# Another order of the experts in a mixture-of-experts layer, and the bias products one place later

## The chip, the cores and the metric

The kernel runs on one core of a Trainium2 chip. The metric is the device time of one execution in microseconds (us). Before the change the median of three runs is 1303.01 us (1302.18 to 1307.84).

## The reference, cut to what matters

One decoder layer on 512 tokens of 1024 channels, all in float32. A mixer (a causal convolution group beside a group of attention heads) is followed by a layer norm, and then by a mixture of experts:

```
logits = x1 @ router_w + router_b            # 32 experts
top4, gates = softmax over the 4 largest logits of each token
for each expert e, on the tokens that chose it:
    g = x1 @ w_gate[e] + b_gate[e];  u = x1 @ w_up[e] + b_up[e]
    h = (clip(u) + 1) * min(g, 7) * sigmoid(1.702 * min(g, 7))
    y = h @ w_down[e] + b_down[e]
out = layer_norm(2**0.25 * x1 + sum over the 4 experts of gate * y)
```

Each expert has three 1024 x 1024 float32 matrices, 12.58 MB. All 32 are read, 403 MB of the 442 MB that the kernel moves.

## The kernel before, in words

The first 271 us compute the mixer, the first layer norm and the router; the change does not touch them. Then comes a loop over 32 places (line 1490 on, `for i, (p, rows) in enumerate(order)`). The experts are sorted by their number of tokens on the chip, and rank p of that order gets a fixed number of rows, `NBLK[p]`. A row is a block of 32 token slots: rank 0 has three, then five ranks have four, seven have three, fifteen two, four one, 78 rows in all. A place is a position in time; `TURNS` says, digit by digit, how many rows the expert at each place has, and `plan()` takes the next free rank with that number. Rows fill groups of four in the order of the places (21 groups); a group can so begin in one place and end in the next.

`expert()` works on a place in six steps. In steps c = 0 to 3 a piece of the gate and up matrices (256 input channels of both, 2.1 MB) is multiplied with the transposed tokens of every row (line 1084); ahead of it stand the bias products of the row (line 1081). After step 3 VectorE and ScalarE compute the activation (`swiglu`, lines 1065 to 1070) and write `hT`. Steps 4 and 5 take a piece of the down matrix each (line 1110 for two rows of one group side by side, line 1113 for a row alone), and the results are copied out as a high and a low part, `yh` and `yl`.

The weights come through SP's queue alone, in the order of the places, six pieces for each place (`expert_loads`, lines 303 and 312). They go to a ring of seven buffers; a piece is issued when the piece seven before it has been used (`advance`). `last_load` (line 1181) takes one of the buffers for good, for the down biases and the rows of the last layer norm: it stands in the stream ahead of the pieces of place `LASTC`, and the ring has six buffers from there.

After each step `tick(c)` lets other work in. At steps 0 and 1 the slots of later groups are worked out (`middle`, `finish`, with the gathers on GpSimd's queue). `fill()` runs one step of the sums: `combine` first makes the selections `cg` on VectorE and then, in eight steps, multiplies them with `yh` and `yl` of two groups, four matmuls of 512 columns a step (line 1154, two matmuls for a single group), and adds the result to `acc`. A combine is put on the list `combs` when the groups are complete. How many steps run is set by `FILLS`: three after step 3 for places of one or two rows, two after steps 0 and 1 for larger ones; in the last places before the end, three after every step. A forced rule clears a combine early when its buffers are wanted again. If the list is empty, nothing runs there. `add_bias` is put on the same list at the end of place `LASTC`: seven steps with the products of the gates with the down biases (line 1339) and the broadcast of the last layer norm's rows (line 1346), 24 matmuls in all. The last place, 31, has one row; the rest of the sums is done in its step 0, and the last layer norm (`outputs`) in steps 1 to 3.

Of the kernel before, what the change touches and what calls it, by code (L numbers as in the profile page):

```python
# [18 lines left out]
T, D, H, E, NE, TOPK = 512, 1024, 8, 64, 32, 4  # L19
# [12 lines left out]

TURNS = "32222422422242223331324231433211"


def plan():

    by = {n: [p for p in range(1, NE) if NBLK[p] == n] for n in (4, 3, 2, 1)}  # L40
    seq = [0] + [by[int(n)].pop(0) for n in TURNS[1:]]
    rows, n = [], 0
# [38 lines left out]
CTAIL, JORD = 4, (4, 5, 6, 7, 0, 1, 2, 3)  # L81
BANKS = (2, 2, 2, 1, 1)
RANK0 = 3.0
LASTC = NE - 4
WARM0, WARM1 = 4, (2, 2, 7)
WARM2 = (0, 0, 0, 14, 0, 0)
XBANKS = ("pu", "pu", "ps", "ps", "pt", "pt", "pu", "pu")
# [2 lines left out]
FILLS = {False: (0, 0, 0, 3, 0, 0), True: (2, 2, 0, 0, 0, 0)}  # L90
# [175 lines left out]
def tile_layer(ctx: ExitStack, tc: tile.TileContext, x, positions, w_in, conv_w, conv_b, conv_ln_g,  # L266
# [792 lines left out]
    def swiglu(st, r, ps):  # L1059
# [10 lines left out]
        V.transpose(st["hT"][:, r].rearrange("p b t -> p (b t)"), um)  # L1070

    def expert(tag, rows, sel, tick, pool=(gd, "gd"), small=lambda: None, keep=False):

        ps = [pool[0].tile([128, 2, 256], F32, name=pool[1]) for _ in rows]
        bv = bT.rearrange("p g (h q j) -> p g h q j", h=2, q=4)
        for c in range(4):
            w = got[tag, "gu", c].rearrange("p g k (h q j) -> p k g h q j", h=2, q=4)
            for i, (st, r) in enumerate(rows):
                if c == 0:
                    for q in range(4):  # L1080
                        P.matmul(ps[i][q * 32:(q + 1) * 32], sel[0:96], bv[:, :, :, q], start=True, stop=False)  # L1081
                for k in range(2):
                    for q in range(4):
                        P.matmul(ps[i][q * 32:(q + 1) * 32], st["xT"][:, r, c * 2 + k], w[:, k, :, :, q], start=False,  # L1084
                                 stop=(c == 3 and k == 1))
                if c:
                    small()
                if c == 3:
                    swiglu(st, r, ps[i])
            advance()  # L1090
            tick(c)
# [10 lines left out]
        for c in range(2):  # L1102
            w = got[tag, "dn", c].rearrange("p k (b q c) -> p k q b c", b=4, q=4)
            for u_, (st, r, n) in enumerate(units):
                d = ds_[u_]
                for k in range(4):
                    kw = dict(start=(c == 0 and k == 0), stop=(c == 1 and k == 3))
                    for j in range(4):
                        if n == 2:
                            P.matmul(d[j * 32:(j + 1) * 32], st["hT"][:, r + j % 2, c * 4 + k],  # L1110
                                     w[:, k, 2 * (j // 2):2 * (j // 2) + 2], **kw)
                        else:
                            P.matmul(d[j * 32:(j + 1) * 32, 0:256], st["hT"][:, r, c * 4 + k], w[:, k, j], **kw)  # L1113
            advance()
            tick(4 + c)
# [25 lines left out]
    def combine(sts):  # L1141

        parts = []
        for st in sts:
            cg = mw.tile([128, T], F32R, name="cg")
            V.tensor_scalar(cg, iota1, st["tk"][:, 0:1], None, op0=OP.is_equal)  # L1146
            parts += [(cg, st[y], st["used"] * 32) for y in ("yh", "yl")]
        yield
        for tt in range(TT):
            for hf in range(2):  # L1150
                c = slice(hf * 512, (hf + 1) * 512)
                ps = cb.tile([128, 512], F32, name="cb")
                for j, (cg, y, n) in enumerate(parts):
                    P.matmul(ps, cg[0:n, tt * 128:(tt + 1) * 128], y[0:n, c], start=(j == 0), stop=(j == len(parts) - 1))  # L1154
                V.tensor_tensor(acc[:, tt, c], acc[:, tt, c], ps, OP.add)  # L1155
                yield
# [31 lines left out]

    stream.insert(len(stream) - 6 * (NE - 1 - LASTC) - 6, last_load)
    GS, combs = {}, []  # L1190

    def begin(i):

        return [(g, s_) for g in range(len(GS), last_group(i) + 1)
                for s_ in [slots(members[g], lambda p, tt: rk1[:, tt, p:p + 1], lambda p, tt: aux[:, tt, p])]
                if next(s_, 0) is None]

    def middle(new):
        for g, s_ in new:
            next(s_)  # L1200

    def finish(new):
        for g, s_ in new:
            GS[g] = dict(next(s_), g=g)

    def ready_x(n):
        for g in range(n + 1):
            if "xT" not in GS[g]:
                xpose(GS[g])

    def fill():
        while combs:
            combs[0][2] -= 1
            if next(combs[0][0], 0) is None:
                return
            combs.pop(0)

    def last_group(i):
        return order[min(i, NE - 1)][1][-1][0]
# [106 lines left out]
    def add_bias():  # L1326

        t = got["last"]
        GT = mw.tile([128, T], F32, name="cg")
        ps = cb.tile([128, 512], F32, name="cb")  # L1330
        for tt in range(TT):
            P.transpose(ps[0:NE, tt * 128:(tt + 1) * 128], Gf[:, tt], ident)
        V.tensor_copy(GT[0:NE], ps[0:NE])
        bdp = t[0:NE, 0].rearrange("p (b q c) -> p q b c", b=4, q=4)
        yield
        for tt in range(TT):
            for hf in range(2):
                ps = cb.tile([128, 512], F32, name="cb")
                P.matmul(ps, GT[0:NE, tt * 128:(tt + 1) * 128], bdp[:, 2 * hf:2 * hf + 2], start=True, stop=True)
                c = slice(hf * 512, (hf + 1) * 512)  # L1340
                V.tensor_tensor(acc[:, tt, c], acc[:, tt, c], ps, OP.add)
            yield
        for i in range(4):
            c = slice(i % 2 * 512, (i % 2 + 1) * 512)
            ps = cb.tile([128, 512], F32, name="cb")
            P.matmul(ps, one1, t[0:1, 2 + i // 2, c], start=True, stop=True)
            S.activation(t[:, i // 2, c], ps, AF.Copy)
            if i % 2:
                yield
# [9 lines left out]
    def overflow():  # L1359

        pcs = cb.tile([128, 512], F32, name="cb")
        for tt in range(TT):
            P.matmul(pcs[:, 0:NE], onesb, mp[:, tt], start=(tt == 0), stop=(tt == TT - 1))
        V.tensor_tensor(ov[:, 0], pcs[:, 0:NE], cap, OP.subtract)
        V.tensor_scalar(ov[:, 1], ov[:, 0], 0.0, None, op0=OP.is_gt)
        for r in range(1, 4):
            V.scalar_tensor_tensor(ov[:, 1], ov[:, 0], 128.0 * r, ov[:, 1], op0=OP.is_gt, op1=OP.add)

        V.tensor_copy(ov[:, 2], ov[:, 1])
        for sft in (1, 2, 4, 8, 16):  # L1370
            V.tensor_copy(ov[:, 3], ov[:, 2])
            V.tensor_tensor(ov[:, 2, sft:NE], ov[:, 3, sft:NE], ov[:, 3, 0:NE - sft], OP.add)
        V.tensor_tensor(ov[:, 1], ov[:, 2], ov[:, 1], OP.subtract)
        V.tensor_copy(nit, ov[0:1, 2, NE - 1:NE])
        yield
# [114 lines left out]
    for i, (p, rows) in enumerate(order):  # L1490
        def tick(c):

            if c == 0:
                middle(new)
            if c == 0 and i == 1:
                combs.append([overflow(), (), 9])
            if c == 1:
                finish(new)
                new.clear()
            if c == 4:  # L1500
                ready_x(last_group(i + 1))
            if c == 5:
                new.extend(begin(i + 1 + LOOK))
            fills = FILLS[len(rows) > 2] if i < NE - 3 else (3, 3, 3, 3, 3, 3)
            if c == 0 and combs and combs[0][1] and combs[0][2] == 9:

                fill()
            if c < 2 and any(g - 3 in k[1] for k in combs for g, r in rows if "yh" not in GS[g]):

                for _ in range(min(3, combs[0][2] - sum(fills[c:]))):  # L1510
                    fill()
            for _ in range(fills[c]):
                fill()

        if i + 1 < NE:
            expert(p, [(GS[g], r) for g, r in rows], selr[:, p] if p else sel0, tick, small=lambda: next(first, 0))
        else:
            break
        if i == LASTC:
            combs.append([add_bias(), (), 9])  # L1520

        ready = order[i + 1][1][0][0] if i + 1 < NE - 1 else ngrp - 1
        while done < ready:
            n = 2 if done < ngrp - 3 else 1
            if done + n > ready:
                break
            combs.append([combine([GS[g] for g in range(done, done + n)]), range(done, done + n), 9])
            done += n
# [64 lines left out]
```

## Time and profile before

| | |
|---|---|
| median of three runs | 1303.01 us |
| profiled execution | 1306.11 us, its span 1304.4 us |
| TensorE (PE) busy | 1227.5 us, 94% of the span |
| VectorE (DVE), ScalarE (ACT), GpSimd (POOL) busy | 46%, 21%, 14% |
| weights queue | 429.98 MB, 81.6% of the 16 DMA engines' span |
| mean granted clock of TensorE | 0.97 of 2.4 GHz |

Start of some places, in us from the start of the span, as the first bias product of the place begins: 2 at 339.2, 3 at 363.3, 6 at 460.3, 8 at 512.0, 12 at 633.0, 16 at 755.1, 17 at 794.3, 19 at 865.4, 21 at 919.1, 22 at 945.4, 26 at 1065.8, 27 at 1117.8, 28 at 1150.9, 29 at 1188.2, 30 at 1228.8, 31 at 1252.0. The rows that each place has are the digits of the old `TURNS`, counted from 0: place 26 has four.

How to read it: busy time counts an instruction from its start to its end, and matmuls overlap, so a busy TensorE can still be slowed by its clock. PEclk is the granted clock, 1.00 for 2.4 GHz and 0.50 for 1.2 GHz. A wait is shown in brackets with what ended it. In a window the columns after the length are the busy us of TensorE's matmuls, TensorE's weight loads, VectorE, ScalarE and GpSimd, with instruction counts, then PEclk, the busy share of the DMA engines and the rate in GB/s.

### The profile page before, as it was taken

Reading aid. Unit: us, or ns where it says so; the run is one execution under the profiler, and the core shown is the slowest. Engines: PE = TensorE matmul, PEld = TensorE weight load, DVE = VectorE, ACT = ScalarE, POOL = GpSimd, SP = SyncE. Lnnn points to the kernel's source line nnn. Section 1 sums busy time; section 2 is a strip of 40 time slices with the busy share of each in tenths; the row PEclk is TensorE's granted clock in tenths of the full one; section 3 lists DMA queues with packets and bytes.
Section 4 is the critical chain, followed back from the end, with each engine's and each line's share of the span. In section 5 each row is a group of like instructions: output and inputs, shape, how many; then the busy total and the mean of one; then the engine's idle time right before and its main releaser. Section 6 shows DMA issues by size and latency. Waiting matters only on the chain. (4 is left out here: it accounts for less than half of the span.)

```text
span 1304.4 us, 25419 instructions
## 1 busy us (share of the span) xinstructions
PE 1227.5 (94%) x10578; PEld 581.5 (45%) x10578; DVE 606.1 (46%) x1444; ACT 280.4 (21%) x551; POOL 185.3 (14%) x158
## 2 busy tenths in 40 slices
PE   8989999889899999999999899999999999999984
PEld 7767767623233343343344334343435334533332
DVE  6999855743433333342333423344234444324464
ACT  5677782311000010010010001110101110101122
POOL 2854101312011011011001110001101101000002
PEclk9999999879899999999999999999999999999877
DMA  9400324679999999999999999999999999899781
GB/s 293 160 1 1 129 82 173 242 279 377 420 420 419 422 419 421 423 415 419 422 419 420 417 419 422 414 405 419 419 421 410 419 422 419 320 351 368 304 362 68
DMA packets 68658, 441.94 MB, mean 339 GB/s; under 512 B 8279, under 2 KB 16615, under 8 KB 27580
## 3 DMA queue, kind: packets, MB, share of 16 engines
q1 hardware_dynamic: 64748, 429.98, 81.6%
q0 software_dynamic: 3792, 10.29, 2.3%
q8 instruction: 85, 1.39, 0.4%
q14 instruction: 33, 0.27, 0.1%
HBM read 435.99 MB, written 4.33 MB: 338 GB/s over the span
## 5 line engine op out<-in xcount | busy, mean ns | idle before, releaser
L1084 PE MATMUL gd<-wt,xTg 128*32 128x512 f32 x4304 | 505.9, 599 | 7.4 <-DMA wt<-in_exp_w_up_dram 5.1
L1084 PEld LDWEIGHTS gd<-wt,xTg 128*32 128x32 f32 x4304 | 158.2, 111 | 288.2 <-issue 268.4
L1110 PE MATMUL gd<-wt,hT 128*32 128x512 f32 x1472 | 192.4, 602 | 15.3 <-DVE hT L1070 12.6
L1020 POOL DMA_INDIRECT xg<-x1d,idx x78 | 74.4, 954 | 864.7 <-DVE tk L1049 820.8
L1066 ACT ACTIVATE sg<-gm 128x256 f32<-128x256 f32 x78 | 32.5, 417 | 618.1 <-DVE gm L1065 616.0
L1065 DVE TENSOR_SCALAR gm<-gd 128x256 f32<-128x256 f32 x77 | 30.9, 402 | 217.1 <-PE gd L1084 211.0
L1128 DVE TENSOR_TENSOR yl<-gd,wh 32x256 fp32r<-32x256 f32 (+1 forms) x104 | 53.4, 513 | 143.3 <-ACT wh L1126 142.3
L1110 PEld LDWEIGHTS gd<-wt,hT 128*32 128x32 f32 x1472 | 58.6, 111 | 130.3 <-issue 95.7
L1126 ACT ACTIVATE wh<-gd 32x256 fp32r<-32x256 f32 (+1 forms) x104 | 46.8, 450 | 195.0 <-PE gd L1110 135.2
L548 PE MATMUL bk<-wt,wh 128*128 128x512 f32 (+1 forms) x352 | 81.2, 378 | 1.4 <-ACT sg L592 0.7
L1155 DVE TENSOR_TENSOR acc<-acc,cb 128x512 f32<-128x512 f32 x88 | 57.6, 678 | 49.9 <-PE cb L1154 49.7
L1113 PE MATMUL gd<-wt,hT 128*32 128x256 f32 x1056 | 73.0, 392 | 4.6 <-issue 2.5
L1084 PE MATMUL gd<-wb,xTg 128*32 128x512 f32 x624 | 76.7, 593 | 0.0
L548 PEld LDWEIGHTS bk<-wt,wh 128*128 128x128 f32 x352 | 61.1, 188 | 14.7 <-ACT sg L592 1.4
L586 DVE SCALAR_TENSOR_TENSOR bk<-u,cT,bk 128x512 f32<-128x512 f32 x88 | 66.2, 753 | 1.8
L1154 PE MATMUL cb<-yl,cg 128*128 128x512 f32 (+2 forms) x160 | 64.7, 404 | 0.0
L1113 PEld LDWEIGHTS gd<-wt,hT 128*32 128x32 f32 x1056 | 42.4, 113 | 32.6 <-issue 15.5
L1154 PE MATMUL cb<-wh,cg 128*128 128x512 f32 (+2 forms) x112 | 48.2, 431 | 5.9 <-DVE cg L1146 5.9
L1081 PE MATMUL gd<-wl,selr 96*32 96x512 bf16 x296 | 49.1, 385 | 0.0
L548 PE MATMUL bk<-wt,wl 128*128 128x512 f32 (+1 forms) x176 | 41.7, 379 | 2.5 <-DVE wl L539 2.1
L1069 DVE SCALAR_TENSOR_TENSOR um<-um,tk,sg 128x256 f32<-128x256 f32 x78 | 39.7, 509 | 8.9
L1128 DVE TENSOR_TENSOR yl<-gd,wl 64x512 fp32r<-64x512 f32 (+1 forms) x36 | 20.5, 570 | 48.8 <-ACT wl L1126 48.5
(340 smaller groups left out, 1292.6 us busy)
## 6 DMA issues: line engine op xcount, KB each, us to landing
wt<-in_exp_w_gate_dram SPq DMA_DIRECT2D x112, 1024.0 KB
wt<-in_exp_w_up_dram SPq DMA_DIRECT2D x112, 1024.0 KB
wt<-in_exp_w_down_dram SPq DMA_DIRECT2D x52, 2048.0 KB
wb<-in_exp_w_down_dram SPq DMA_DIRECT2D x12, 2048.0 KB
wb<-in_exp_w_gate_dram SPq DMA_DIRECT2D x16, 1024.0 KB
wb<-in_exp_w_up_dram SPq DMA_DIRECT2D x16, 1024.0 KB
wt<-in_w_in_dram SPq DMA_DIRECT2D x3, 2048.0 KB
acc<-in_x_dram SPq DMA_DIRECT2D x8, 512.0 KB
```

What stands on the lines that cost most here:

```text
L548: P.matmul(b.t[:, ts], w.t[:, k], xx[:, k, ts], start=(pas == 0 and k == 0), stop=(pas == 2 and k == KT - 1))
L586: op("V", 0.663, (lambda j: lambda e: V.scalar_tensor_tensor(b.t, u[:, c, j:j + T], cT[:, c, j:j + 1], b.t, op0=OP.mult, op1=OP.add))(j), ...
L1020: G.indirect_dma_start(out=xg[:, r], out_offset=None, in_=x1d[:, :], in_offset=bass.IndirectOffsetOnAxis(ap=idx[:, r:r + 1], axis=0))
L1069: V.scalar_tensor_tensor(um, um, st["tk"][:, 8 + r:9 + r], sg, op0=OP.mult, op1=OP.mult)
L1081: P.matmul(ps[i][q * 32:(q + 1) * 32], sel[0:96], bv[:, :, :, q], start=True, stop=False)
L1084: P.matmul(ps[i][q * 32:(q + 1) * 32], st["xT"][:, r, c * 2 + k], w[:, k, :, :, q], start=False, stop=(c == 3 and k == 1))
L1110: P.matmul(d[j * 32:(j + 1) * 32], st["hT"][:, r + j % 2, c * 4 + k], w[:, k, 2 * (j // 2):2 * (j // 2) + 2], **kw)
L1113: P.matmul(d[j * 32:(j + 1) * 32, 0:256], st["hT"][:, r, c * 4 + k], w[:, k, j], **kw)
L1126: S.activation(st["yh"][o], a, AF.Copy)
L1128: V.tensor_tensor(st["yl"][o], a, st["yh"][o].bitcast(F32), OP.subtract)
L1154: P.matmul(ps, cg[0:n, tt * 128:(tt + 1) * 128], y[0:n, c], start=(j == 0), stop=(j == len(parts) - 1))
L1155: V.tensor_tensor(acc[:, tt, c], acc[:, tt, c], ps, OP.add)
```

## The change

The string that orders the places is another one, with the same digits. `LASTC` is 29 instead of 28: the small loads stand ahead of place 29's pieces, six pieces later, and the bias products go on the list after place 29. The rule of three steps of the sums after every step holds for place 30 alone, not for 29 and 30.

```
-TURNS = "32222422422242223331324231433211"
+TURNS = "32233222414213421342232224322321"
...
-LASTC = NE - 4
+LASTC = NE - 3
...
-            fills = FILLS[len(rows) > 2] if i < NE - 3 else (3, 3, 3, 3, 3, 3)
+            fills = FILLS[len(rows) > 2] if i < NE - 2 else (3, 3, 3, 3, 3, 3)
```

## Rows read from the trace of the kernel before

**Rows 1.** The page: span, busy share of TensorE, and 40 slices of the transfers.
```profile
span 1304.4 us, 25419 instructions
...
PE 1227.5 (94%) x10578; PEld 581.5 (45%) x10578; DVE 606.1 (46%) x1444; ACT 280.4 (21%) x551; POOL 185.3 (14%) x158
...
DMA  9400324679999999999999999999999999899781
GB/s 293 160 1 1 129 82 173 242 279 377 420 420 419 422 419 421 423 415 419 422 419 420 417 419 422 414 405 419 419 421 410 419 422 419 320 351 368 304 362 68
```

**Rows 2.** Timeline of TensorE: start, duration (us), instructions; in brackets the wait before them.
```profile
756.73 1.92 PE L1084 MATMUL gd<-wt,xTg 128*32 128x512 f32 x16 [1.20 <-DMA wt<-in_exp_w_up_dram]
...
881.67 0.64 PE L1084 MATMUL gd<-wt,xTg 128*32 128x512 f32 x4 [1.40 <-DMA wt<-in_exp_w_up_dram]
...
1068.72 0.64 PE L1084 MATMUL gd<-wt,xTg 128*32 128x512 f32 x4 [2.51 <-DMA wt<-in_exp_w_up_dram]
```

**Rows 3.** Windows by place: length, busy us of PE PEld DVE ACT POOL, PEclk, DMA.
```profile
339.20:363.30 24.10, 22.24 (x207) 6.51 (x202) 7.36 (x17) 2.02 (x4) 0.00 (x0) 1.00 1.01 419
460.30:486.10 25.80, 25.39 (x234) 9.98 (x230) 10.35 (x32) 2.02 (x4) 3.79 (x4) 1.00 1.01 414
512.00:557.10 45.10, 45.10 (x415) 17.60 (x411) 14.67 (x35) 4.03 (x8) 0.00 (x0) 1.00 1.02 424
633.00:676.30 43.30, 43.30 (x427) 17.07 (x423) 11.70 (x30) 4.04 (x8) 3.79 (x4) 1.00 1.02 420
...
794.30:832.00 37.70, 36.92 (x360) 14.52 (x357) 15.59 (x40) 4.73 (x12) 0.00 (x0) 1.00 1.02 423
865.40:879.90 14.50, 14.50 (x164) 7.10 (x157) 10.00 (x25) 2.47 (x6) 0.00 (x0) 1.00 1.01 423
...
919.10:945.40 26.30, 24.16 (x300) 10.61 (x297) 9.15 (x23) 4.29 (x11) 3.78 (x4) 0.94 1.01 418
945.40:987.50 42.10, 42.10 (x468) 18.83 (x464) 15.68 (x42) 5.93 (x15) 0.00 (x0) 1.00 1.01 423
1065.80:1117.80 52.00, 49.49 (x508) 23.45 (x504) 17.26 (x51) 5.86 (x14) 3.79 (x4) 0.97 1.00 411
1117.80:1150.90 33.10, 32.32 (x347) 13.05 (x343) 11.85 (x32) 4.26 (x11) 1.90 (x2) 1.00 0.87 326
1150.90:1188.20 37.30, 36.98 (x350) 14.50 (x345) 13.24 (x32) 3.10 (x7) 0.00 (x0) 1.00 0.91 342
1188.20:1228.80 40.60, 39.67 (x333) 16.83 (x330) 16.91 (x37) 6.71 (x15) 0.95 (x1) 0.96 0.81 308
1228.80:1252.00 23.20, 18.76 (x154) 8.31 (x150) 11.34 (x23) 1.94 (x6) 0.00 (x0) 0.85 1.01 424
1252.00:1304.40 52.40, 30.55 (x206) 14.69 (x198) 29.59 (x58) 14.96 (x24) 11.38 (x5) 0.72 0.40 163
```

**Rows 4.** Timeline of TensorE in place 16 and at the down products of place 21.
```profile
763.62 0.47 PE L1154 MATMUL cb<-wl,cg 128*128 128x512 f32 x1 [1.00 <-DVE cg L1146]
...
764.16 0.39 PE L1154 MATMUL cb<-wh,cg 128*128 128x512 f32 x1
764.39 0.39 PE L1154 MATMUL cb<-yl,cg 128*128 128x512 f32 x1
...
936.84 0.65 PE L1113 MATMUL gd<-wt,hT 128*32 128x256 f32 x4 [2.14 <-DVE hT L1070]
```

**Rows 5.** Windows before place 16 and behind two waits (columns as in rows 3).
```profile
744.00:756.70 12.70, 8.42 (x72) 2.12 (x69) 6.79 (x24) 2.01 (x4) 0.00 (x0) 1.00 1.01 414
936.80:940.20 3.40, 3.36 (x32) 1.80 (x36) 3.06 (x6) 0.42 (x1) 0.00 (x0) 0.50 1.01 408
1069.90:1073.30 3.40, 3.40 (x24) 1.30 (x20) 0.00 (x0) 0.00 (x0) 0.00 (x0) 0.51 1.01 422
```

**Rows 6.** Timeline of SP's queue at one issue, and the window behind it.
```profile
1123.97 0.37 SPq L303 DMA_DIRECT2D wt<-in_exp_w_gate_dram  x1
...
1124.00:1125.00 1.00, 1.00 (x12) 0.37 (x8) 0.22 (x2) 0.00 (x0) 0.00 (x0) 1.00 0.35 74
```

## The prediction

> **What bounds the kernel now.** I read the page first: the matrix engine is busy for 94% of the span, and the transfer lines show 9 (90% or more) and about 420 GB/s from the 11th to the 34th of the 40 slices [rows 1]. Two resources are full at once, so the page alone does not say which one sets the time. The next view is TensorE's timeline around the starts of places, where a wait for a weight piece can be seen. The reader is to see three waits: places 16, 20 and 26 begin their weight matmuls at 756.73, 881.67 and 1068.72 us, each just after a DMA of the second half of their first piece [rows 2]. These are clock readings of the transfer stream: (1068.72 - 756.73) / 10 = 31.2 us per place, whatever the place holds, since every expert has the same 12.6 MB. TensorE's time depends on the rows instead: in the windows by place, one row takes 14.5 us, two about 25.8, three 37.5, four 42 to 45 with the sums that are mixed in [rows 3]. So two-row and one-row places run down the lead of the transfers, three-row and four-row places build it up. Where the lead reaches zero, the stream sets the time; after the last such point TensorE alone does. In the old order that last point is place 26: from 1068.7 on the transfers are ahead (from 1117.8 they move 308 to 342 GB/s, because they wait for buffers [rows 3]), and TensorE needs 1304.4 - 1068.7 = 235.7 us to the end.
>
> **The change part by part: the order.** The rows, the pieces, the sums (21 groups, 16 matmuls each) are the same in number, so what counts is where the stream last binds and what TensorE has left there. Stream times for the new order follow from the 31.2: place 13 at 756.7 - 3 x 31.2 = 663.1, place 17 at 787.9, place 25 at 1037.5.
>
> TensorE's time for the new places is put together from old windows of the same shape [rows 3], 0.23 us being added for each matmul of the sums more (two of them start 0.23 apart, [rows 4]). Which place has which sums I counted from the code: a combine has one step that makes the selections and eight of four matmuls.
>
> - Places 3 to 12, from 363.3: 37.3, 37.7, 24.1 (two rows, no sums left, as old place 2), 25.8, 25.8, 45.1, 14.5, 47.8 (old 26 without its 2.5 us DMA wait [rows 2] and 1.7 of clock [rows 5]), 26.3 (as old 21), and 15.5 for a single row without sums (14.5 as old 19, less 12 x 0.23, with the wait of 2.1 and the clock fall of 1.7 told of below): 299.8, so place 13 at 663.1. The stream gives 663.1.
> - 13 to 16: 37.7, 43.3 + 16 x 0.23 = 47.0, 26.3, 14.5: 125.5, place 17 at 788.6. The stream gives 787.9.
> - 17 to 24: 38.6, 43.3, 25.8, 27.6, 33.1, 25.8, 25.8, 24.1: 244.1, so TensorE would reach place 25 at 1032.7. The stream gives 1037.5: it binds here.
>
> After place 25 come 3, 2, 2, 3, 2 and 1 rows: 13 in six places, and the lead grows to about 12 us at place 26 and stays above 10. So place 25 is the last point, one place sooner than in the old order, with 17 rows to go instead of 14. TensorE's rest from there:
>
> - 25: 42.1 as old 22, less 0.2 before its first weight matmul: 41.9.
> - 26: 37.3 as old 28, and 16 matmuls of the sums more (3.7), and 1.0 for the selections, which are made in the same step (the wait of [rows 4]): 42.0.
> - 27 and 28: two rows each, both in different groups, and the list of sums is empty, as in old 21: 26.3 each, 52.6.
> - 29: 37.7 as old 17.
> - 30: 40.6 as old 29, whose bias products it takes over, and 12 more of the sums (2.8): 43.4.
> - 31: 52.4, and 1.0 for four more matmuls of the sums ahead of the last normalization, at half clock for part of it: 53.4.
>
> Sum 271.0. That is 35.3 more than the old 235.7, against 31.2 that the stream saves by binding a place sooner: 1037.5 + 271.0 = 1308.5, or +4.1.
>
> The windows of 27 and 28 need a word. In old place 21 nothing covers the activation of the last row: TensorE waits 2.14 us for hT at 936.84 [rows 4], and right behind it the granted clock is 0.50, the lower level, from 936.8 to 940.2 [rows 5]. That costs 1.7 us and is in the 26.3. The wait for the DMA at place 26 has the same sequel from 1069.9 on. The waits before place 16, 4.3 us in all from 744.0 to 756.7, had none, the clock stayed at 1.00 [rows 5]; so a fall is likely behind a wait of 2.1 and not sure. Without any, 27 and 28 are 3.3 us cheaper.
>
> **Two terms without a row of their own.** First, whether place 25 itself starts with a clock fall, as old 26 did: 0 to 1.7, I take 0.8. Second, the ring. A piece is issued when the piece seven before it has been used. Places 3 and 4 now have three rows each, so at place 5 the transfers lead by 438.3 - 413.5 = 25 us (place 5's first piece at 756.7 - 11 x 31.2), and the last pieces of place 5 and the first of place 6 are issued within about 1 us of when the stream could start them. An issue that finds the stream empty moves little in its first microsecond (74 GB/s after the issue at 1123.97, [rows 6]). So the stream, which then stays late up to place 25, loses between nothing and some 4 us; I take 2, the middle. A gain is excluded, since it was at 420 GB/s there before. Together: 1308.5 + 0.8 + 2 = 1311.3, which is 6.9 over the old span. The profiled execution took 1306.1 with a span of 1304.4, the median of the runs is 1303.0; I add the difference to the median: **1310**.
>
> On the stream's rate the rows show 411 to 424 GB/s over whole places [rows 3]. The Trainium skill, "DMA: Bandwidth & Descriptors", Specifications, gives a limit of about 358 GB/s for what a core draws from HBM. By an estimate from that page a place would take 12.58 MB / 358 = 35.1 us, binding one place sooner would save 35.1 instead of 31.2, and the result would be no change; the trace disagrees, and the row is used.
>
> **The bias products and the steps.** The load of the bias and the last layer norm's rows takes a ring buffer for good, now ahead of place 29 instead of 28. There the transfers are ahead by over 10 us in either case, so one buffer more during place 28 is worth nothing. SP issues the same three small DMAs six pieces later. The 24 bias matmuls keep their length and their place on the path (TensorE does nothing else meanwhile); old place 29 and new place 30 both have two rows to mix them with, and they cover the activation there. Three steps in every part of place 30 instead of places 29 and 30: the first six steps of group 18's sums, which old place 30 had beside its gate and up products, run in new place 30's down part, with the selections made ahead of it. This is the part that gains, and it is in the terms: old place 30 with its single row cost 23.2 us, 4.4 of them idle and the clock at 0.85 on the mean [rows 3], and I give new place 30 none of that beyond what old 29 had.
>
> **Rivals.**
> - No fall of the clock at 25, 27 and 28 and no loss in the ring: 1037.5 + 271.0 - 3.3 = 1305.2, 0.8 over, 1304. For it: the waits before place 16. Against: the falls at 936.8 and 1069.9.
> - Faster: the stream doesn't bind at place 25. Without the falls in 11, 12 and 15 TensorE reaches it at 1032.7 - 3 x 1.65 = 1027.8, and 271.0 - 3.3 more give 1295.5, 8.9 under: 1294.1. It decides if place 25's first piece lands before 1028, 9 us sooner, or 0.4 us per place from place 3 on. Against it: the stream is full in the whole stretch [rows 1], and the bytes are the same.
> - Much slower: the stream runs empty for longer (4 us), and the starved places 23 to 25, with waits at each piece, let the clock fall in 25 and again in 26, with a microsecond lost at each later place whose selections come late: 1308.5 + 4 + 1.7 + 4 = 1318, less 1.4 for the median: 1317.
>
> **Numbers.** Forecast 0.50 (1306 to 1314), no fall and no loss 0.25, faster 0.08, much slower 0.17. A measurement can tell 0.5%, 6.5 us, from no change: slower is above 1309.5, faster below 1296.5. The forecast's own range is two thirds above 1309.5: slower 0.33 + 0.17 = 0.50, same 0.17 + 0.25 = 0.42, faster 0.08. Range 1299 to 1317: it leaves out the faster rival and the upper half of the slow one.
>
> **What would show it.** Right: first weight matmul of place 25 at 1037 to 1041, behind DMA waits; small DMA waits at 13 and 17; waits of 2.1 us ahead of the down products of 27 and 28 with PEclk at 0.50 behind them; place 31 from 1257 on instead of 1252.0; GB/s below 420 near 440 us. Wrong: TensorE reaches place 25 without a DMA wait, or a later place waits for a piece, or the stretch from place 25 to the end is more than 5 us off 271.

## The result, and the profile after

The changed kernel takes **1312.58 us** (median of 20 runs, 1308.41 to 1322.58), the kernel before 1304.67 (20 runs beside it, 1301.14 to 1310.03 and one of 2506.01); the ratio is 1.0069, with a 95% interval of 1.0051 to 1.0087. So it is slower by 0.7%, about 8 us. The profiled execution took 1313.37 us, with a span of 1311.4.

The page of the changed kernel, the lines that answer to [rows 1]:

```profile
span 1311.4 us, 25985 instructions
...
PE 1226.0 (93%) x10834; PEld 591.3 (45%) x10834; DVE 615.6 (47%) x1476; ACT 287.8 (22%) x575; POOL 185.6 (14%) x158
...
GB/s 291 159 1 1 129 94 160 240 307 391 420 422 370 386 420 419 421 422 424 419 418 419 370 391 419 421 408 419 418 419 418 420 421 402 391 408 422 353 183 68
```

TensorE's busy time is the same (1226.0 us against 1227.5), although it has 256 matmuls more, since more rows have no neighbour of their place in the group (line 1113); the 7 us are idle time (85.4 us against 76.9). The rate has two dips that were not there before, 370 and 386 in the 13th and 14th slice (393 to 459 us) and 370 and 391 in the 23rd and 24th (721 to 787 us). They cover places 4 and 5, and 14 to 16.

Timeline of TensorE in the changed kernel, where places 13, 17 and 25 begin their weight matmuls (columns as in rows 2), and the down products of rows alone in places 27 and 28:

```profile
668.14 2.79 PE L1084 MATMUL gd<-wt,xTg 128*32 128x512 f32 x12 [3.41 <-DMA wt<-in_exp_w_up_dram]
...
797.05 2.52 PE L1084 MATMUL gd<-wt,xTg 128*32 128x512 f32 x12 [3.73 <-DMA wt<-in_exp_w_up_dram]
...
1045.23 1.92 PE L1084 MATMUL gd<-wt,xTg 128*32 128x512 f32 x16 [1.21 <-DMA wt<-in_exp_w_up_dram]
...
1145.30 1.93 PE L1113 MATMUL gd<-wt,hT 128*32 128x256 f32 x32 [1.10 <-issue]
1147.43 0.42 PE L1113 MATMUL gd<-wt,hT 128*32 128x256 f32 x4 [0.20 <-DVE hT L1070]
...
1168.06 1.93 PE L1113 MATMUL gd<-wt,hT 128*32 128x256 f32 x32 [0.70 <-DVE hT L1070]
```

Place 25 is the last that waits for a weight piece, at 1045.23 us; TensorE needs 1311.4 - 1045.2 = 266.2 us from there. Before, it was place 26 at 1068.7, with 235.7 us left [rows 2]. The stream is 23.5 us sooner at its last binding point, and what is left there is 30.5 us more: +7.0, the difference of the spans.

Windows by place of the changed kernel (columns as in rows 3): 4, 14, then 25 from its first weight matmul, and 26 to 31:

```profile
401.10:439.20 38.10, 37.32 (x382) 15.09 (x379) 13.59 (x33) 4.82 (x12) 3.79 (x4) 1.00 0.93 350
707.10:754.40 47.30, 47.30 (x496) 22.59 (x493) 18.15 (x44) 6.39 (x15) 0.00 (x0) 1.00 0.95 386
...
1045.20:1087.10 41.90, 41.87 (x394) 17.09 (x398) 13.19 (x33) 2.85 (x6) 0.00 (x0) 1.00 1.01 423
1087.10:1129.00 41.90, 40.66 (x382) 18.28 (x378) 14.67 (x34) 3.06 (x7) 3.78 (x4) 1.00 0.98 389
1129.00:1152.60 23.60, 22.30 (x280) 9.76 (x277) 8.96 (x22) 4.30 (x11) 0.00 (x0) 1.00 1.00 409
1152.60:1175.40 22.80, 21.85 (x278) 8.46 (x274) 9.09 (x31) 3.80 (x11) 1.90 (x2) 1.00 1.01 401
1175.40:1213.30 37.90, 36.30 (x354) 13.78 (x347) 15.21 (x40) 4.37 (x12) 0.95 (x1) 1.00 1.01 422
1213.30:1258.90 45.60, 44.67 (x266) 16.64 (x258) 18.65 (x35) 5.70 (x11) 0.00 (x0) 0.93 0.84 336
1258.90:1311.40 52.50, 32.06 (x207) 15.24 (x206) 31.41 (x60) 13.13 (x20) 11.44 (x5) 0.72 0.21 83
```

Two things are to be seen. In place 4 the transfers move 350 GB/s where the full stream moves 420: the stream waits for buffers. By the issues on SP's queue and the trace's semaphore events, the fourth piece of place 5 was issued at 423.0 us, when a buffer came free, just as the piece before it landed (423.4); it landed at 432.8, 9.4 us after that one, where the full stream brings one every 5.2 (31.2 us per place). And places 27 and 28 take 23.6 and 22.8 us at full clock, not the 26.3 each that the forecast took from old place 21 [rows 3].

### The profile page after: what moved, and what is told of

Its sections match the earlier page's. It is cut to its first block, busy times and chain, and to the rows that moved or that the text cites. A ratio compares the mean times of both kernels' runs of the same rounds, so it can differ in the third digit from the quotient of the medians.

```text
span 1311.4 us, 25985 instructions
## 1 busy us (share of the span) xinstructions
PE 1226.0 (93%) x10834; PEld 591.3 (45%) x10834; DVE 615.6 (47%) x1476; ACT 287.8 (22%) x575; POOL 185.6 (14%) x158
## 5 line engine op out<-in xcount | busy, mean ns | idle before, releaser
L1084 PE MATMUL gd<-wt,xTg 128*32 128x512 f32 x4272 | 498.0, 597 | 11.2 <-DMA wt<-in_exp_w_up_dram 9.7
L1084 PEld LDWEIGHTS gd<-wt,xTg 128*32 128x32 f32 x4272 | 154.7, 110 | 286.6 <-issue 267.2
L1110 PE MATMUL gd<-wt,hT 128*32 128x512 f32 x1408 | 185.4, 610 | 13.0 <-DVE hT L1070 7.5
L1110 PEld LDWEIGHTS gd<-wt,hT 128*32 128x32 f32 x1408 | 59.2, 112 | 118.1 <-issue 81.7
L1113 PE MATMUL gd<-wt,hT 128*32 128x256 f32 x1568 | 102.6, 385 | 9.1 <-issue 5.5
L1113 PEld LDWEIGHTS gd<-wt,hT 128*32 128x32 f32 x1568 | 62.1, 111 | 48.6 <-issue 17.8
L1128 DVE TENSOR_TENSOR yl<-gd,wl 32x256 fp32r<-32x256 f32 (+1 forms) x54 | 26.5, 490 | 61.3 <-ACT wl L1126 60.8
L1084 PEld LDWEIGHTS gd<-wb,xTg 128*32 128x32 f32 x656 | 25.3, 110 | 41.5 <-issue 38.7
```

The costliest lines, as they stand in the source:

```text
L1128: V.tensor_tensor(st["yl"][o], a, st["yh"][o].bitcast(F32), OP.subtract)
```

## The experiments

**The order alone, and the rest alone.** The change has two parts. The first kernel has the new `TURNS` with the old `LASTC` and steps; the second the old `TURNS` with the new ones:

```
-LASTC = NE - 3                                    # order alone
+LASTC = NE - 4
-            fills = ... if i < NE - 2 else ...
+            fills = ... if i < NE - 3 else ...

-TURNS = "32233222414213421342232224322321"        # the rest alone
+TURNS = "32222422422242223331324231433211"
```

> New order alone; the load of the bias, the bias products and the three steps after every part stay where they were (ahead of place 28, places 29 and 30). Theory (the stream of weights binds at place 25 and loses time at places 4 to 6 and 14 to 16, because the ring is full): first weight matmul of place 25 at 1045 us within 2, as in the changed kernel; the whole loss is there or more, 1310 to 1318 us. Rival (the bias products and the steps in the last places make the loss): 1302 to 1306 us.

> Old order with the new place of the bias load and products and the steps after every part in place 30 alone. Theory (stream): place 26 begins at 1068.7 within 2 as before; the end does not get longer, and may gain: old place 30 (one row, 23.2 us with 4.4 of waits and the clock at 0.85) is covered by the bias products, so 1296 to 1304 us. Rival (the end makes the loss): 1309 to 1314 us.

Measured: the order alone 1312.62 us (6 runs), ratio 1.0062 [1.0040, 1.0085]; the rest alone 1303.69 (12 runs), 1.0000 [0.9977, 1.0024]. The order carries the whole loss. The bias products and the steps move time between places: with the new order alone, place 29 took 59.7 and place 30 30.3 us, 90.0 together, against 83.5 in the changed kernel's first profile and 86.8 in a second one (below); in the medians nothing of that is left that could be told from zero. Two expectations on single profiles failed: place 26 of the old order with the rest alone began its weight matmuls at 1064.65 us, not within 2 of 1068.7, and place 25 with the order alone not within 2 of 1045:

```profile
1040.53 1.92 PE L1084 MATMUL gd<-wt,xTg 128*32 128x512 f32 x16 [1.20 <-DMA wt<-in_exp_w_up_dram]
```

That is place 25 of the kernel with the order alone (timeline of TensorE): the same place binds, 4.7 us sooner than in the changed kernel's profile. Nothing of either edit acts before place 28, so the last binding point moves by 4 to 5 us from one execution to the next, in either order.

**A stream that cannot bind.** In both kernels the down pieces are loaded by half from the third place on; the other half of each buffer keeps old values, so this is not the layer's output, only its time without a full stream:

```
+                n = 2048 if count[0] > 14 else 4096
-                SP.dma_start(t.rearrange("p k f -> p (k f)"),
+                SP.dma_start(t.rearrange("p k f -> p (k f)")[:, 0:n],
-                             ...rearrange("e (p k) f -> p (e k f)", k=4))
+                             ...rearrange("e (p k) f -> p (e k f)", k=4)[:, 0:n])
```

> Old kernel with half of each down piece loaded from the 15th piece on (the other half keeps what the buffer held), so that the stream needs about 26 us a place instead of 31.2 and can't bind. Theory (stream): TensorE's own chain is left, the span of before less its waits for weights (1.2 + 1.4 + 2.5 and about 2 in place 15) and one clock fall: 1294 to 1298 us. Rival (uncovered activations or the end make the difference of the two orders): the same time for this kernel, but 7 to 8 us below the next one.

> Changed kernel with half of each down piece loaded from the 15th piece on (the other half keeps what the buffer held). Theory (stream): without its waits for weights (2.3 + 3.4 in places 12 and 13, 3.7 in 17, about 4 in 24 and 25) and two clock falls behind them the changed kernel comes to 1293 to 1298 us, within 3 us of the old order under the same cut. Rival (uncovered activations of places 5, 11, 12, 15, 27, 28, or the end, make the loss): 1301 to 1306 us, 7 to 8 us above the old order under the same cut.

Measured: 1280.12 us for the old order (ratio 0.9814 [0.9792, 0.9837]) and 1282.18 for the new one (0.9823 [0.9798, 0.9848]), 5 runs each. Without a binding stream the intervals of the two orders overlap, and the 7.9 us between the medians shrink to 2.1: the loss is in the stream, not in the ends of the places (a rest of a few us is not excluded). Both gained more than was expected (1294 to 1298 and 1293 to 1298). Groups of TensorE's instructions by line in the old order with half loads (busy us, mean ns, idle us before them and what ended it):

```profile
L1085 PE MATMUL gd<-wt,xTg 128*32 128x512 f32 x4304 | 498.7, 596 | 2.0 <-DVE xTg L1057 2.0
L1111 PE MATMUL gd<-wt,hT 128*32 128x512 f32 x1472 | 183.9, 599 | 9.3 <-DVE hT L1071 7.3 <-PE gd L1085 1.5 <-PE cb L1364 0.5
```

(Lines are one higher here.) No wait for a DMA is left. Place 26 starts 21.6 us sooner than before (1044.2 against 1065.8), and 16.7 of these lie behind the start of place 3 (358.4 against 363.3), though the visible waits for `wt` in the kernel before were 5.1 us; the section on the hardware comes back to that.

**Where the stream loses.** Places 4 and 5 of the new order have 3 and 2 rows; here they are exchanged (`TURNS` 3223**32**... becomes 3223**23**..., all else as in the changed kernel):

```
-TURNS = "32233222414213421342232224322321"
+TURNS = "32232322414213421342232224322321"
```

> The changed kernel with places 4 and 5 of the order exchanged (3 and 2 rows become 2 and 3), nothing else; the rows left behind every later place are the same. Theory (the ring runs full at place 4 and empties the stream): with two rows in place 4 the transfers lead by 17 us instead of 28 at place 5, no issue finds the stream empty there, the first pieces of places 5 and 6 land 31 us apart instead of 38.1, and every later stream point comes 5 to 7 us sooner: place 13 at 658 to 662 (664.3 to 668 in the changed kernel), the first weight matmul of place 25 at 1038 to 1040 instead of 1045.2, and the span 1305 to 1307, median 1304 to 1308. Rival (the stream is slow there for a reason of its own, such as what the other queues carry at 420 to 450 us): the landing gap stays near 38, place 25 stays at 1045, median 1312. Rival (the loss is made up elsewhere, place 25 being late through places 14 to 17): 13 comes sooner, 25 does not.

Measured: 1308.20 us (12 runs), ratio 1.0042 [1.0019, 1.0065]. Windows of places 4 and 5, and place 25's first weight matmul in the timeline:

```profile
398.30:425.00 26.70, 26.70 (x316) 12.35 (x313) 10.49 (x26) 4.24 (x11) 3.78 (x4) 1.00 1.01 416
425.00:457.60 32.60, 31.82 (x333) 10.91 (x329) 12.14 (x30) 4.35 (x12) 0.00 (x0) 1.00 1.01 421
```
```profile
1041.31 1.92 PE L1084 MATMUL gd<-wt,xTg 128*32 128x512 f32 x16 [1.20 <-DMA wt<-in_exp_w_up_dram]
```

The dip at place 4 is gone (416 and 421 GB/s), and the first pieces of places 5 and 6 landed 32.2 us apart, by the trace's semaphore events, against 38.0. Place 25 came 3.9 us sooner than in the first profile of the changed kernel, at 1041.3, not the 1038 to 1040 expected, and the span was 1310.4, not 1305 to 1307. The kernel with the order alone, which has 3 rows in place 4, was at 1040.5 as well, with a gap of 31.1. So the loss at place 4 is not a fixed property of the order, and the intervals of the two ratios overlap: that the exchange gains anything is not shown.

**The changed kernel once more**, nothing altered:

> The changed kernel again, nothing altered, for a second profiled execution. Theory: the loss of the stream at places 4 to 6 is no fixed property of the order but follows TensorE's arrival at place 3: if that is at 363 or later the gap of the first pieces of places 5 and 6 is 36 to 38 and place 25 starts at 1043 to 1046; if at 360 or sooner, the gap is 31 to 32 and place 25 starts at 1038 to 1041. Rival: the gap is 38 whatever the arrival.

One run, 1310.91 us, with a span of 1308.9. Windows of places 4, 27, 28 and 30, and the start of place 25:

```profile
396.20:434.30 38.10, 37.32 (x382) 15.07 (x379) 13.58 (x33) 4.82 (x12) 3.78 (x4) 1.00 0.99 402
...
1123.30:1146.90 23.60, 22.29 (x284) 9.72 (x281) 8.96 (x22) 4.30 (x11) 0.00 (x0) 1.00 0.99 408
1146.90:1169.70 22.80, 21.86 (x281) 8.46 (x277) 9.08 (x31) 3.81 (x11) 1.89 (x2) 1.00 1.01 402
1207.60:1256.50 48.90, 47.97 (x270) 17.02 (x264) 18.73 (x35) 5.85 (x11) 0.00 (x0) 0.86 0.78 313
```
```profile
1039.50 1.92 PE L1084 MATMUL gd<-wt,xTg 128*32 128x512 f32 x16 [1.19 <-DMA wt<-in_exp_w_up_dram]
```

Place 3 began at 358.9 here (363.7 in the first profile), place 4 moved 402 GB/s instead of 350, the gap of the first pieces of 5 and 6 was 31.3, and place 25 began its weight matmuls at 1039.5. All three are as the theory has them: the loss follows TensorE's arrival. TensorE's rest, 1308.9 - 1039.5 = 269.4, is 3.2 more than in the first profile, all of it in place 30 (48.9 against 45.6).

Why TensorE came late in the first profile can be read from place 2, which holds 4.1 of the 4.8 us. Its window in the first profile, the waits ahead of its down products there (timeline of TensorE), and its window in the second:

```profile
335.00:363.70 28.70, 25.50 (x224) 7.64 (x220) 7.47 (x19) 2.02 (x4) 3.79 (x4) 0.88 1.01 417
```
```profile
352.81 1.06 PE L1110 MATMUL gd<-wt,hT 128*32 128x512 f32 x2 [2.14 <-issue]
354.94 9.36 PE L1110 MATMUL gd<-wt,hT 128*32 128x512 f32 x59 [1.07 <-DVE hT L1070]
```
```profile
334.30:358.90 24.60, 22.74 (x228) 7.40 (x224) 7.47 (x19) 2.02 (x4) 3.78 (x4) 1.00 1.01 415
```

In the first profile the granted clock was at 0.50 from 353.6 to 360.4 us, behind the wait of 2.14 us; that costs 3.4 us. In the second the waits were 0.75 and 1.11 us, and the clock stayed at 1.00. The first piece of place 5 landed at nearly the same time in both (411.8 and 412.4). So a clock fall made TensorE late against an equal stream, and 6.7 us of the stream were lost behind it. Why the first wait was longer in one execution was not settled.

What the gap goes by is the lead, the time from the landing of place 5's first piece to TensorE's start of that place. With leads of 21.9 to 22.1 us (second profile, order alone, and the exchange of 11 and 29 below) the gap is 31.1 to 31.3, with 27.4 in the first profile it is 38.0, and with two rows in place 4 (leads of 11 to 12) 32.0 to 32.2. The loss is not made up: from the first piece of place 6 to that of place 25 the stream took 594 to 596 us in all seven profiles of the new order and its exchanges, and 592.8 in the kernel before.

**A delay of 5.8 us at place 3, in both orders.** The bias matmuls of the first row are issued 25 times (the last issue alone counts):

```
                 if c == 0:
-                    for q in range(4):
-                        P.matmul(ps[i][...], sel[0:96], bv[:, :, :, q], start=True, stop=False)
+                    for e in range(24 if tag == order[3][0] and i == 0 else 0, -1, -1):
+                        for q in range(4):
+                            P.matmul(ps[i][...], sel[0:96], bv[:, :, :, q], start=True, stop=e > 0)
```

> The changed kernel with TensorE delayed by some 6 us at the start of place 3: the four bias matmuls of its first row are issued 25 times instead of once (24 x 0.24 = 5.8 us; the last four alone count in the output). Theory (a full ring hands TensorE's lateness on to the stream): place 4 and 5 start 6 us later, the transfers' lead there grows past what seven buffers hold, the first pieces of places 5 and 6 land 36 to 44 us apart, and the first weight matmul of place 25 comes at 1045 to 1052, so the whole delay or most of it is still there at the end: 1315 to 1319, 3 to 6 us over the changed kernel. Rival (what TensorE loses ahead of the last binding point is repaid there, as in any order): place 25 stays at 1040 to 1045, the median at 1312 to 1313.

> The kernel before with the same delay of 5.8 us at the start of place 3. There the transfers lead by 10 to 15 us at places 3 and 4, and the ring is not full. Theory: the stream does not notice; the visible DMA waits of places 16, 20 and 26 (1.2, 1.4, 2.5) shrink or go, since TensorE comes later, and place 26 starts its weight matmuls at 1068 to 1071; median 1303 to 1306 (ratio 1.0 to 1.002). Rival (the stream binds too little in the old order, so a delay is added in full): 1308 to 1310.

Measured: new order 1314.68 us (6 runs), 1.0082 [1.0060, 1.0104]; old order 1304.33 (12 runs), 0.9998 [0.9983, 1.0012]. The new order with the delay, place 4 and the start of place 25:

```profile
404.10:442.10 38.00, 37.22 (x379) 14.99 (x376) 13.54 (x33) 4.76 (x12) 3.79 (x4) 1.00 0.91 346
```
```profile
1047.89 1.50 PE L1085 MATMUL gd<-wt,xTg 128*32 128x512 f32 x12 [1.19 <-DMA wt<-in_exp_w_up_dram]
```

In the new order the delay reaches the stream: 346 GB/s in place 4, a gap of 38.1, a lead of 27.7 at place 5, and place 25 at 1047.9, 8.4 us after the second profile; 2.0 of these were there at the first piece of place 5 already, 6.8 came with the gap, and 0.4 went again behind it. In the median it is 2 us over the changed kernel, between the two expectations, and the intervals overlap: shown in the trace, not in the time. In the old order the delay costs nothing in the median, as the theory had it. Its place 26 came at 1064.1, below the 1068 to 1071 expected (the old order with the rest alone had 1064.65 without a delay), and its DMA wait did not shrink. The lead in the profile before was 11.2 us at place 3 and 5.9 at place 4, not 10 to 15.

```profile
1064.12 1.93 PE L1085 MATMUL gd<-wt,xTg 128*32 128x512 f32 x16 [2.91 <-DMA wt<-in_exp_w_up_dram]
```

**A row moved from behind the last binding point to ahead of it.** Places 11 and 29 of the changed kernel are exchanged:

```
-TURNS = "32233222414213421342232224322321"
+TURNS = "32233222414313421342232224322221"
```

> The changed kernel with places 11 and 29 of the order exchanged (2 and 3 rows become 3 and 2), nothing else. Theory (the stream sets the time up to place 25, and what TensorE has left there sets the rest): a row of computing moves from behind the last point where the stream binds to ahead of it, where it takes the place of waiting. Place 25 starts its weight matmuls at the same 1043 to 1046, the DMA wait at place 13 (3.4) is gone, and the rest is 266.2 less a row's 12, 253 to 256: span 1298 to 1301, median 1297 to 1301, ratio 0.995 to 0.998. Rival (places are bound by TensorE everywhere, and the order matters through its covers): a row costs the same at 11 and at 29, and the median stays at 1312. Rival (with two rows at 27 to 30 in sequence the stream binds once more, at place 30 or 31): DMA waits there, median 1303 to 1306.

Measured: **1295.84 us** (9 runs), ratio 0.9945 [0.9923, 0.9966]. Place 25 in the timeline, and the windows of 11 and 29 and 30:

```profile
1035.91 1.07 PE L1084 MATMUL gd<-wt,xTg 128*32 128x512 f32 x8 [1.21 <-DMA wt<-in_exp_w_up_dram]
```
```profile
614.20:646.90 32.70, 31.83 (x337) 16.36 (x333) 11.70 (x28) 4.26 (x11) 0.00 (x0) 1.00 1.01 419
...
1169.20:1193.70 24.50, 24.50 (x221) 8.61 (x217) 8.72 (x24) 2.02 (x4) 0.95 (x1) 1.00 1.01 422
1193.70:1242.40 48.70, 45.81 (x260) 15.94 (x254) 17.88 (x32) 5.84 (x11) 0.00 (x0) 0.86 0.98 402
```

Place 29 takes 24.5 us instead of 37.9, place 11 takes 32.7 instead of the 23.0 (second profile) or 25.7 it needs with two rows, and that extra is not paid: the waits ahead of 12 and 13 are gone, and place 14 begins 342.0 us after place 3, as it does in the second profile of the changed kernel. The rest from place 25 is 1292.4 - 1035.9 = 256.5, as expected within 0.5 (253 to 256). Place 25 itself was expected at 1043 to 1046 and came at 1035.9, since TensorE was early at place 3 (356.9) and the ring lost nothing at place 4 (gap 31.1). With that the span (1292.4) and the median are below what was expected (1298 to 1301 and 1297 to 1301).

**Both exchanges.**

```
-TURNS = "32233222414213421342232224322321"
+TURNS = "32232322414313421342232224322221"
```

> The changed kernel with both exchanges, 4 with 5 and 11 with 29: 32232322414313421342232224322221. If the two effects are apart (4 and 5: the ring at the start; 11 and 29: a row moved ahead of the binding point): 1290 to 1296, 0 to 4 us under the exchange of 11 and 29 alone (1295.8). Place 25 at 1033 to 1040, a rest of 253 to 257. Rival (the exchange of 4 and 5 gains nothing where place 13 no longer binds): 1295 to 1297.

Measured: 1295.57 us (6 runs), 0.9921 [0.9901, 0.9941]; place 25 at 1040.5 and a rest of 1297.3 - 1040.5 = 256.8. The exchange of 4 and 5 adds nothing that can be told.

**An order searched for.**

```
-TURNS = "32233222414213421342232224322321"
+TURNS = "31232422412431233242242233232221"
```

> The changed kernel with an order of places searched with a recurrence of landings and uses (piece lands 5.2 us after the one before it, or 9 us after its issue; two-row places 25.8, three 37.5, four 43 to 45): 31232422412431233242242233232221. By the theory the transfers never lead by more than 21 us from place 4 on (so the ring does not run the stream empty), they bind last at place 15 and barely at 31, and the computing that is left behind that has no wait: median 1285 to 1297 (0.98 to 0.99 of the kernel before). If stream waits turn out at places 20 to 31 as well, 1297 to 1305. Rival (only the number of rows behind the last binding point counts, and any order ends within 1300 to 1312 for reasons not in the recurrence, such as falls of the clock behind uncovered activations): 1303 or more.

Measured: **1293.90 us** (8 runs), 0.9933 [0.9910, 0.9955]. It beats both kernels, as do the two before it; the three cannot be told apart. Its last waits for a piece:

```profile
1177.33 3.64 PE L1084 MATMUL gd<-wt,xTg 128*32 128x512 f32 x32 [1.43 <-DMA wt<-in_exp_w_up_dram]
...
1192.59 1.92 PE L1084 MATMUL gd<-wt,xTg 128*32 128x512 f32 x16 [1.21 <-DMA wt<-in_exp_w_up_dram]
```

Here the stream binds up to place 30, at 1192.6, and 98.7 us are left of the span of 1291.3: places 30 and 31. The median is in the range expected, but not for the reason given: the last bound was to be at place 15, and with waits at places 20 to 31 the expectation was 1297 to 1305.

## Why the prediction was right, point by point

The forecast was 1310 us, slower; measured are 1312.58, on the same side and 2.6 over. Of these 1.7 are the starting point: the forecast added its 6.9 us to a median of 1303.01, and the kernel before has 1304.67 over 20 runs. All profiles with full loads beside each other, as "last point where the stream binds + TensorE's rest = span":

| kernel | last binding point | rest | span | median ratio |
|---|---|---|---|---|
| before | 1068.7 (place 26) | 235.7 | 1304.4 | 1 |
| the rest alone (old order) | 1064.7 (26) | 233.9 | 1298.6 | 1.0000 |
| old order, delay | 1064.1 (26) | 233.7 | 1297.8 | 0.9998 |
| forecast | 1039.5 (25) | 271.8 | 1311.3 | |
| changed, first profile | 1045.2 (25) | 266.2 | 1311.4 | 1.0069 |
| changed, second profile | 1039.5 (25) | 269.4 | 1308.9 | |
| order alone | 1040.5 (25) | 272.7 | 1313.2 | 1.0062 |
| 4 and 5 exchanged | 1041.3 (25) | 269.1 | 1310.4 | 1.0042 |
| new order, delay | 1047.9 (25) | 264.4 | 1312.3 | 1.0082 |
| 11 and 29 exchanged | 1035.9 (25) | 256.5 | 1292.4 | 0.9945 |
| both exchanges | 1040.5 (25) | 256.8 | 1297.3 | 0.9921 |
| searched order | 1192.6 (30) | 98.7 | 1291.3 | 0.9933 |

- **What bounds the kernel.** Right, and shown from two sides: without a binding stream the two orders are within 2.1 us, and a row moved ahead of the binding point saves about its own length behind it (269.4 or 266.2 against 256.5).
- **Place 25 as the last binding point, one place sooner.** Right in every profile of the new order with full loads. That TensorE would be 4.8 us early there was far too little: with half loads it began place 25 at 1015.3 us, not at the forecast 1032.7. From place 3 on that is 656.5 us instead of 669.4, and 6.7 of the 12.9 lie in places 11 and 15, taken like 27 and 28 below from old place 21.
- **The loss in the ring.** The mechanism was right, the size not: 2 us were taken with bounds of 0 and 4. In the first profile place 25 was 7.7 us after the 1037.5 of a stream that loses nothing, beyond the upper bound; in the second it was 2.0. Counted on the stream itself, from the first piece of place 5 to that of place 25, the loss against the kernel before (623.5 us) was 9.8 and 3.5. What sets it is the lead, and so TensorE's arrival at place 3, which lay between 356.9 and 363.7 us in the profiles of the new order, and which the prediction took as fixed (363.3, a lead of 25). It also looked at places 4 and 5 alone, while the rate dips at 14 to 16 as well (386 GB/s in place 14, a dip in the 23rd and 24th slice in both profiles); that this has the same cause was not tested.
- **Places 27 and 28.** 52.6 was forecast, 46.4 measured in both profiles: TensorE was idle for 0.9 to 1.3 us in each instead of 2.1 at one wait, and no clock fall came. The step that failed is the use of one old window (place 21) as a property of the kernel. In the old kernel with the delay the same place 21 took 23.7 us. The fall that was costed at 0.8 in place 25 did not come either (41.9 us at 1.00).
- **Place 30.** 43.4 forecast, 45.6 and 48.9 measured; with the clock's share taken out (0.93 of 45.6 means 6.4 us at half clock, 3.2 lost; 0.86 of 48.9 means 6.8 lost) it is 42.4 and 42.1. The work was sized right, the clock falls in the place of the bias products were left out.
- **Places 26, 29 and 31.** 42.0, 37.7 and 53.4 forecast; 41.9, 37.9 and 52.5 measured.
- **The bias and the steps.** They were said to be the part that gains. Alone, they are worth nothing in the old order; in the new one the places they touch got shorter by 3.2 and 6.5 us in the two profiles, and the medians (1312.58 and 1312.62) don't show it.

So the sum of the first profile (1311.3 forecast, 1311.4 measured) owes its closeness to luck, two misses of opposite sign: the stream 5.7 late, the rest 5.6 short. In the second profile the stream came when forecast, and the rest was 2.4 short. The direction did not depend on them: the rest grew by 28.7 to 33.7 in the profiles of the changed kernel with or without delay, the stream's gain was 20.8 to 29.2, and in each profile the first was the larger. Of the signs that the prediction named, the DMA waits at 13 and 17 (3.41 and 3.73 us, not small), place 31 from 1257 on (1258.9 and 1256.5) and the dip near 440 us came, place 25 at 1037 to 1041 came in the second profile alone, and the waits and clock falls of 27 and 28 did not come.

## What to carry to other kernels

Where a stream of equal pieces and work of unequal length take turns in setting the time, look for the last point where the stream binds: what is left to compute there sets the end, and work moved ahead of that point is free as long as it fills waits. Long places early make the lead large; where it comes near what the ring holds, lateness of the compute engine is handed on to the stream, which does not catch up. A wait or a clock fall seen in one profile is a value of that execution; a second profile of the same kernel shows which of them are not fixed.

## What the runs showed of the hardware that was not expected

**Waits for `hT` and waits for pieces trade with each other.** Old order, groups of the down products of two rows side by side; first the kernel before, then the one with the delay (where the line is one higher):

```profile
L1110 PE MATMUL gd<-wt,hT 128*32 128x512 f32 x1472 | 192.4, 602 | 15.3 <-DVE hT L1070 12.6 <-issue 1.9 <-PE gd L1084 0.7
```
```profile
L1111 PE MATMUL gd<-wt,hT 128*32 128x512 f32 x1472 | 185.8, 607 | 10.8 <-DVE hT L1070 6.2 <-DMA wt<-in_exp_w_down_dram 3.3 <-PE gd L1085 0.7
```

The same instructions waited 12.6 us for `hT` in one execution and 6.2 in another; places of two rows took about 25.8 us in the first [rows 3] and 24.6 to 25.2 in the second where no piece was late. With the stream as the bound, what is not lost there seems to be lost in front of the next piece: the groups of the delayed kernel show 14.4 us of waits for pieces, those of the kernel before 5.1. So the 5.1 us of DMA waits in the profile before were much less than what the stream cost, which the half loads showed (24 us in the median). The activation of the first row began 15.4 us after the start of places 7 and 10 in the kernel before, and 13.1 us after it in the old order with the rest alone; why it is later in some executions was not settled. Products of the next piece stand between those of the piece before it in the timeline of the kernel before (at 609 to 612 us, the start of place 11), but place 11 had its activation after 13.5 us, so that alone does not explain it.

**The clock falls in the place of the bias products.** It stood at 0.96 in old place 29 [rows 3], at 0.93 and 0.86 in new place 30, and at 0.89 and 0.78 where only one part of the change was made, although TensorE waited only 0.8 to 0.9 us in these places (2.5 in the last of them). In the first profile of the changed kernel the products with the down biases stand from 1227.2 to 1238.5 us, others between them, and the clock was at 0.50 from 1237.7 to 1241.1 and from 1247.9 to 1251.3. No run was made to settle what does it.
